# Up-projections of three MLPs in pairs of output tiles, by seven products of half tiles

## The chip, the cores and the metric

The kernel runs on one core of a Trainium2 chip. Its time is the device time of one execution in microseconds, as the median of several runs; less is better. The core has TensorE for matmuls, VectorE, ScalarE and GpSimd for elementwise work, and a queue on SyncE (SP) that issues the DMAs. Each engine takes its own instructions in order; engines wait for each other by semaphores.

## The reference, cut to what matters

Four layers, each a mixer (retention, convolution, gated linear attention, retention) and an MLP, with norms and residuals, on 512 tokens of 1024 features in float32:

```python
def sq_relu_mlp(u, w_up, w_down):
    return jnp.square(jax.nn.relu(u @ w_up)) @ w_down

h = x
for i in range(4):
    u = rmsnorm(h, norm_gains[i, 0])
    y = mixer(i, u)
    h = h + rmsnorm(y, norm_gains[i, 1])
    u = rmsnorm(h, norm_gains[i, 2])
    h = h + rmsnorm(sq_relu_mlp(u, mlp_w_up[i], mlp_w_down[i]), norm_gains[i, 3])
return h
```

Here w_up is 1024 x 4096 and w_down 4096 x 1024 in each layer.

## The kernel before

Activations lie transposed: features on the 128 partitions, the 512 tokens along the free axis. A 1024 x 512 activation is eight tiles of 128 x 512. For nearly the precision of float32, each operand is split into two tiles of type fp32r, hi (the value cast) and lo (the rest), and a product is three matmuls into one accumulator in PSUM: hi x hi, hi x lo, lo x hi (`mm3`, L392 to L394).

Weights come as panels of 128 x 1024, each the eight k-blocks of one output tile, in the order of use (`Stream`). `prep` loads a panel into a raw tile (L130, tag wraw, three buffers), casts it to hi on ScalarE (L137) and subtracts on VectorE for lo (L138). The ring of hi and lo tiles has six slots of each. `next` calls for panels up to three ahead.

In an MLP the 4096 hidden features are worked in four blocks of 1024 (b = 0 to 3). A block has eight up-projections, whose outputs become the eight tile pairs act, and then eight down-projections, which read all eight act pairs in order k = 0 to 7 and are added to the outputs y. An up-projection (`proj`) is 8 x 3 matmuls of 512 columns into one PSUM bank of seven. It is evacuated by `up`: VectorE takes the maximum with 0 times the norm factor r (L542), ScalarE squares (L543) and casts to hi (L373), VectorE subtracts for lo (L380). A down-projection is evacuated by ScalarE in block 0 (L246) and added by VectorE in the others (L251). Block 0 begins with four output tiles at once, in halves of 256 columns, while the norm is still being worked out (`lead`). Block 3 ends with four down-projections in halves of 256 columns (`trail`); their panels lie in four pairs of tiles of the MLP's own pool (tag w, eight buffers) instead of the ring, so that the next layer's panels can be cut early.

The operand X of the up-projections is h times a gain per feature, split into hi and lo by the `Close` of the mixer; the norm factor r comes in only at the evacuation. `tmp` tiles are a ring of four.

TensorE's instructions run in the order in which the program is written. Those of the other engines are ordered beforehand by a planner, which plays the program through in time: an instruction may be put ahead of earlier ones that are not ready. Tiles of a pool are released when their last reader is through.

Of the kernel before, what the change touches and what calls it, by code (L numbers as in the profile page):

```python
# [1 line left out]

# [1 line left out]

# [16 lines left out]
P = 128  # L21
# [72 lines left out]
class Stream:  # L94


    def __init__(self, K, src, ahead):
        self.K, self.src, self.ahead = K, src, ahead
        self.n = src.shape[0]
        self.ready, self.loaded, self.at = [], 0, 0  # L100
        self.aside = {}
        self.cut = {}

    def ring(self):
        K = self.K
# [1 line left out]

    def prep(self, parts=1):

        if self.loaded >= self.n:  # L110
            return []
        K = self.K
        nc = K.nc
        i = self.loaded
        self.loaded += 1
        if i in self.cut:
            hi, lo = self.aside.pop(i, self.ring)()
            pan = Panel(hi, lo)
            self.ready.append(pan)
            for tiles, src in zip((hi, lo), self.cut[i]):  # L120
                for t, x in enumerate(tiles):
                    nc.sync.dma_start(x.bitcast(F32), src[:, t * pan.w:(t + 1) * pan.w])
            return []
        raw = K.wp.tile([P, 8 * P], F32, name="wraw", tag="wraw", bufs=3)
        hi, lo = self.aside.pop(i, self.ring)()
        pan = Panel(hi, lo)
        self.ready.append(pan)

        def load(a, b):
            nc.sync.dma_start(raw[:, a:b], self.src[i][:, a:b])  # L130

        def split(a, b):
            for c in range(a, b, min(pan.w, b - a)):
                d = c + min(pan.w, b - a)
                t, o = divmod(c, pan.w)
                h, l = (x[t][:, o:o + d - c] for x in (hi, lo))
                nc.scalar.activation(h, raw[:, c:d], AF.Copy)  # L137
                nc.vector.tensor_tensor(l, raw[:, c:d], h.bitcast(F32), ALU.subtract)  # L138

        if parts == 1:  # L140
            load(0, 8 * P)
            split(0, 8 * P)
        else:
            w = 8 * P // parts
            return [(lambda a=a: load(a, a + w), lambda a=a: split(a, a + w)) for a in range(0, 8 * P, w)]

    def cut_early(self, i, pool):

        K = self.K
        nc = K.nc  # L150
        raw = K.wp.tile([P, 8 * P], F32, name="wraw", tag="wraw", bufs=3)
        nc.sync.dma_start(raw, self.src[i])
        hi, lo = (pool.tile([P, 8 * P], F32R, name="early", tag="early", bufs=2) for _ in range(2))
        nc.scalar.activation(hi, raw, AF.Copy)
        nc.vector.tensor_tensor(lo, raw, hi.bitcast(F32), ALU.subtract)
        self.cut[i] = [K.tc.dram_tile([P, 8 * P], F32, name=f"cut{n}{i}") for n in "hl"]
        for d, t in zip(self.cut[i], (hi, lo)):
            nc.sync.dma_start(d, t.bitcast(F32))

    def next(self, ahead=None):  # L160
        ahead = self.ahead if ahead is None else ahead
        while len(self.ready) < 1 + ahead and self.loaded < self.n:
            self.prep()
        self.at += 1
        return self.ready.pop(0)

# [3 lines left out]
            self.aside[self.at + first + i] = fn  # L170

    def fill(self, n):
        while len(self.ready) < n and self.loaded < self.n:
            self.prep()

    def group(self, n, ahead=0):
# [6 lines left out]
def _spare(pool, tag, bufs, w=8 * P):  # L183

    def alloc():
        return [[pool.tile([P, w], F32R, name=f"w{tag}", tag=tag, bufs=bufs) for _ in range(8 * P // w)] for _ in range(2)]
    return alloc
# [44 lines left out]
class Close:  # L232
# [26 lines left out]
    def half(self, c):  # L259
        K, nc = self.K, self.K.nc  # L260
        a, b = c
        if self.r is None:
            self.r = K.rp.tile([P, T], F32, name="ro", tag="ro", bufs=1)
            if self.nxt is not None:
                K.X = K.new_x()
        K.rsqrt(self.r, self.sum.mean(c), c)
        ts = {}
        with K.tc.manual_schedule(engines={DVE}):
            for k in range(KD + 2):
                if k < KD:  # L270
                    ts[k] = K.tmp()
                    nc.vector.scalar_tensor_tensor(ts[k][:, a:b], self.ys[k][:, a:b], K.gain(self.layer, self.which, k), self.r[:, a:b], ALU.mult, ALU.mult)  # L272
                if 1 <= k <= KD:
                    hk = K.h[k - 1][:, a:b]
                    nc.vector.tensor_tensor(hk, hk, ts[k - 1][:, a:b], ALU.add)  # L275
                    if self.nxt is None:
                        nc.sync.dma_start(K.out[(k - 1) * P:k * P, a:b], hk)
                    else:
                        K.split_hi(K.X[k - 1], hk, c, K.gain(*self.nxt, k - 1))
                if k >= 2 and self.nxt is not None:  # L280
                    K.split_lo(K.X[k - 2], K.h[k - 2][:, a:b], c, K.gain(*self.nxt, k - 2))
            if b == T and self.late:
                K.norm_sums()


class Kern:
# [99 lines left out]
        self.split_hi(pr, src, c, scale)  # L386
        self.split_lo(pr, src, c, scale)

    def mm3(self, out, A, B, start, stop):

        mm = self.nc.tensor.matmul
        mm(out, lhsT=A[0], rhs=B[0], start=start, stop=False)  # L392
        mm(out, lhsT=A[0], rhs=B[1], start=False, stop=False)  # L393
        mm(out, lhsT=A[1], rhs=B[0], start=False, stop=stop)  # L394
        self.tick(3 * (out.shape[-1] / 2400 + 0.0025))
# [122 lines left out]
            self.after(5.0 if c[1] == T else 2.5, lambda c=c: close.half(c))  # L518


    def mlp(self, close, early=()):
        nc = self.nc
        FB = 4
        early = list(early)
        steps = 0

        def step():

            nonlocal steps
            steps += 1  # L530
            if early and steps % 2 == 0:
                self.W.cut_early(early.pop(0), mp)

        with self.tc.tile_pool(name="mlp", bufs=1) as mp:
            self.W.keep(FB * 2 * KD - 4, [_spare(mp, "w", 8)] * 4)
            for b in range(FB):
                act = [self.pair(mp, "act", 2 * KD) for _ in range(KD)]

                def up(n, ps, c):
                    lo, hi = c  # L540
                    t = self.tmp()
                    nc.vector.scalar_tensor_tensor(t[:, lo:hi], ps[:, lo:hi], 0.0, self.r[:, lo:hi], ALU.max, ALU.mult)  # L542
                    nc.scalar.activation(t[:, lo:hi], t[:, lo:hi], AF.Square)  # L543
                    self.split(act[n], t[:, lo:hi], c)

                n0 = 0
                if b == 0:
                    n0 = 4
                    self.lead(n0, up)
                for n in range(n0, KD):  # L550
                    ps = self.proj()
                    self.when(lambda n=n, ps=ps: up(n, ps, (0, T)))
                    step()

                def down(n, ps, c):
                    if b == 0:
                        close.first(n, ps)
                    else:
                        close.add(n, ps, c)

                n1 = KD - 4 if b == FB - 1 else KD
                for n in range(n1):
                    down(n, self.proj(act), (0, T))
                    step()
                    if b == FB - 1:
                        close.done(n)
                if n1 < KD:
                    pan = self.W.group(4, 4)
                    self.trail([([pan[i].blk(k) for k in range(KD)], act, n1 + i) for i in range(4)], down, close)
# [794 lines left out]
    def run(self):  # L1364
        self.taps = [(0, 10)] * 2 + [(6, 10)] * 2 + [(7, 10)] * 2 + [(10, 8), (28, 0)]
        self.shift_at = 60.0
        self.side = 6
        self.fin = 2.0, 7.0, 7.0, 2.0
        self.ends = HALVES
        self.norm_at, self.tok_at = 22.0, 4.5  # L1370
        self.first_norm()
        for layer in range(DEPTH):
            kind, j = layer % 3, layer // 3
            close = Close(self, layer, 1, (layer, 2), True)
            if kind == 0:
                self.retention(layer, j, close)
            elif kind == 1:
                self.conv(layer, close)
            else:
                self.gla(layer, close)  # L1380
            last = layer + 1 == DEPTH
            early = range(self.W.at + N_MLP, self.W.at + N_MLP + N_CONV) if kind == 0 and not last else ()
            self.mlp(Close(self, layer, 3, None if last else (layer + 1, 0), not last and (layer + 1) % 3 == 0), early)
        self.flush()


# [136 lines left out]
```

## Time and profile before

| | us |
|---|---|
| median of 3 runs | 2761.25 |
| lowest and highest | 2756.51, 2762.49 |
| the profiled execution | 2758.31 |
| its span in the trace | 2756.6 |

| engine | busy us | share of the span | instructions |
|---|---|---|---|
| TensorE matmuls (PE) | 2695.5 | 98% | 13298 |
| TensorE weight loads (PEld) | 2277.9 | 83% | 13298 |
| VectorE (DVE) | 1637.7 | 59% | 2517 |
| ScalarE (ACT) | 1191.4 | 43% | 1801 |
| GpSimd (POOL) | 134.8 | 5% | 133 |

The shares are averages over stages with different limits. Weight loads run beside matmuls. The duration of one matmul in the trace contains the time it takes to drain, in which the next one already runs; how fast matmuls follow each other is read from their starts. An idle time is put down to the event that ended it.

### The profile page before, as it was taken

To read this page: it belongs to the slowest core of one execution; us is meant where nothing else is said; L and a number is where in the kernel's file an instruction comes from. 1 tells how busy PE (TensorE), PEld (TensorE's weight loads), DVE (VectorE), ACT (ScalarE), POOL (GpSimd) and SP (SyncE) were. 2 spreads that over 40 slices of the span, in tenths; PEclk is the share of its full clock that TensorE was granted. 3 is DMA by queue.
4 is the path that set the end of the run, shared out by engine and by line. 5 is a ranking of instruction groups with operands and counts; after the bars stand their busy time and mean duration, and the time that the engine had idled before them with its cause. 6 is when DMAs were issued, how large, how long until landed. Compare 5 with 4: busy or idle time off the path is not lost.

```text
span 2756.6 us, 33440 instructions
## 1 busy us (share of the span) xinstructions
PE 2695.5 (98%) x13298; PEld 2277.9 (83%) x13298; DVE 1637.7 (59%) x2517; ACT 1191.4 (43%) x1801; POOL 134.8 (5%) x133
## 2 busy tenths in 40 slices
PE   8999999999999699999999999999999999999998
PEld 7888888788898498888887888888888888988887
DVE  7755568455459974444688684345665555844444
ACT  5443445434337554332377554233443443543322
POOL 4000000000009400000000000000000000000000
PEclk9999999999999799999999999999999999999999
DMA  5222233766544003223122222323212222132231
GB/s 175 77 75 94 74 102 108 250 234 247 207 166 155 16 32 115 100 92 105 63 70 77 82 95 92 100 97 124 69 62 92 84 69 97 57 115 94 98 100 46
DMA packets 82670, 289.98 MB, mean 105 GB/s; under 512 B 9169, under 2 KB 11473, under 8 KB 82513
## 3 DMA queue, kind: packets, MB, share of 16 engines
q1 hardware_dynamic: 82368, 287.77, 30.9%
q8 instruction: 104, 1.70, 0.2%
q14 instruction: 54, 0.43, 0.0%
q10 hardware_dynamic: 144, 0.07, 0.0%
HBM read 260.02 MB, written 27.79 MB: 104 GB/s over the span
## 4 chain that ended last, share of the span: by engine, by line
PE 86%; DVE 8%; POOL 2%; ACT 2%; issue 1%; DMA 1%; SPq 0%; DVEq 0%; POOLq 0%; ACTq 0%
PE ps L393 28%; PE ps L394 28%; PE ps L392 28%; POOL y L897 2%; DVE wlo L138 1%; DVE ps L912 1%; DVE acc L210 1%; DMA wraw<-in_wst_dram 1%; DVE tmp L272 0%; DVE h L275 0%; PE st L218 0%; ACT whi L137 0%; DVE actl L380 0%; PE st L228 0%; DVE y L927 0%
## 5 line engine op out<-in xcount | busy, mean ns | idle before, releaser
L137 ACT ACTIVATE whi<-wraw 128x1024 fp32r<-128x1024 f32 (+1 forms) x396 | 414.3, 1049 | 820.3 <-PE ps L393 734.5
L392 PE MATMUL ps<-xh,whi 128*128 128x512 f32 (+1 forms) x1984 | 738.2, 372 | 3.9 <-DVE tmp L542 3.0
L393 PE MATMUL ps<-xl,whi 128*128 128x512 f32 (+1 forms) x1984 | 735.6, 371 | 1.1 <-DVE xl L382 1.1
L394 PE MATMUL ps<-xh,wlo 128*128 128x512 f32 (+1 forms) x1984 | 735.1, 371 | 0.0
L138 DVE TENSOR_TENSOR wlo<-wraw,whi 128x1024 fp32r<-128x1024 f32 (+1 forms) x396 | 483.3, 1223 | 218.3 <-ACT whi L137 213.6
L392 PEld LDWEIGHTS ps<-xh,whi 128*128 128x128 f32 x1984 | 374.9, 189 | 68.6 <-issue 3.8
L393 PEld LDWEIGHTS ps<-xl,whi 128*128 128x128 f32 x1984 | 374.8, 189 | 66.1 <-DVE xl L382 1.7
L394 PEld LDWEIGHTS ps<-xh,wlo 128*128 128x128 f32 x1984 | 374.9, 189 | 63.3
L393 PE MATMUL ps<-actl,whi 128*128 128x512 f32 x896 | 350.1, 391 | 1.4 <-DVE actl L380 1.3
L392 PE MATMUL ps<-acth,whi 128*128 128x512 f32 x896 | 349.0, 390 | 0.5 <-ACT acth L373 0.5
L394 PE MATMUL ps<-acth,wlo 128*128 128x512 f32 x896 | 348.9, 389 | 0.0
L251 DVE TENSOR_TENSOR y<-y,ps 128x512 f32<-128x512 f32 (+1 forms) x200 | 114.8, 580 | 319.0 <-PE ps L394 318.7
L542 DVE SCALAR_TENSOR_TENSOR tmp<-ps,rx 128x512 f32<-128x512 f32 x128 | 86.9, 689 | 227.2 <-PE ps L394 226.9
L393 PEld LDWEIGHTS ps<-actl,whi 128*128 128x128 f32 x896 | 168.3, 188 | 40.5 <-DVE actl L380 5.8
L392 PEld LDWEIGHTS ps<-acth,whi 128*128 128x128 f32 x896 | 168.3, 188 | 36.0 <-ACT acth L373 0.9
L394 PEld LDWEIGHTS ps<-acth,wlo 128*128 128x128 f32 x896 | 168.3, 188 | 34.0
L210 DVE TENSOR_TENSOR acc<-acc,sq 128x256 f32<-128x256 f32 (+1 forms) x245 | 118.6, 487 | 51.4 <-ACT sq L209 45.5
L392 PE MATMUL ps<-whi,xh 128*128 128x512 f32 (+1 forms) x384 | 138.3, 360 | 6.9 <-ACT whi L137 5.8
L393 PE MATMUL ps<-wlo,xh 128*128 128x512 f32 (+1 forms) x384 | 137.1, 357 | 0.0
L394 PE MATMUL ps<-whi,xl 128*128 128x512 f32 (+1 forms) x384 | 137.1, 357 | 0.0
L209 ACT ACTIVATE sq<-y 128x256 f32<-128x256 f32 (+1 forms) x105 | 46.9, 456 | 126.7 <-DVE y L251 105.0
L380 DVE TENSOR_TENSOR actl<-tmp,acth 128x512 fp32r<-128x512 f32 x128 | 87.6, 690 | 4.1 <-ACT acth L373 4.0
(321 smaller groups left out, 3835.7 us busy)
## 6 DMA issues: line engine op xcount, KB each, us to landing
wraw<-in_wst_dram SPq DMA_DIRECT2D x438, 512.0 KB, 3.5
cuth<-early SPq DMA_DIRECT2D x24, 512.0 KB, 2.6
cutl<-early SPq DMA_DIRECT2D x24, 512.0 KB, 3.0
whi<-cuth SPq DMA_DIRECT2D x20, 512.0 KB, 3.9
wlo<-cutl SPq DMA_DIRECT2D x20, 512.0 KB, 4.7
h<-in_xT_dram SPq DMA_DIRECT2D x8, 256.0 KB, 5.4
wraw<-in_wst_dram SPq DMA_DIRECT2D x8, 256.0 KB, 5.4
ww<-cuth SPq DMA_DIRECT2D x4, 512.0 KB, 6.3
```

The costliest lines, as they stand in the source:

```text
L137: nc.scalar.activation(h, raw[:, c:d], AF.Copy)
L138: nc.vector.tensor_tensor(l, raw[:, c:d], h.bitcast(F32), ALU.subtract)
L209: nc.scalar.activation(t, src, AF.Square, scale=scale)
L210: nc.vector.tensor_tensor(acc, acc, t, ALU.add)
L251: self.K.nc.vector.tensor_tensor(y, y, ps[:, a:b], ALU.add)
L380: self.nc.vector.tensor_tensor(lo, src, hi, ALU.subtract)
L392: mm(out, lhsT=A[0], rhs=B[0], start=start, stop=False)
L393: mm(out, lhsT=A[0], rhs=B[1], start=False, stop=False)
L394: mm(out, lhsT=A[1], rhs=B[0], start=False, stop=stop)
L542: nc.vector.scalar_tensor_tensor(t[:, lo:hi], ps[:, lo:hi], 0.0, self.r[:, lo:hi], ALU.max, ALU.mult)
L897: nc.gpsimd.tensor_tensor(co[i], co[i], o, ALU.add)
L912: nc.vector.scalar_tensor_tensor(sums[i], x, w, sums[i], ALU.mult, ALU.add)
```

## The change

In layers 1, 2 and 3 the up-projections of blocks 1 to 3 are made in pairs of output tiles. The two output tiles of 128 features and the 512 tokens make a 2 x 2 matrix of blocks (feature tile by half of the tokens), the 1024 input features are cut in two halves of four k-blocks, and the product of 2 x 2 blocks is made by seven products (Strassen's scheme, in Winograd's form) in place of eight. Each product has 4 k-blocks x 3 matmuls of 256 columns.

The operands: `combos` makes four combinations of the halves of X in block 0's down-phase, from h and the gain, and splits them into the eight tiles of tag w that the last four down panels also use. `Stream.pair` loads the two panels of a pair and makes the four combinations of their halves on VectorE; it gives four entries of the ring, three of two blocks each and one of one block, each cut into hi and lo. The first entry is cut at once, the others in `steps` as the stream is asked for them. `seven` asks for panels five ahead (`deep`), accumulates products into three PSUM banks where they are summed anyway, copies four partial sums out by ScalarE, adds by VectorE, and calls `up` with the sums in SBUF. `mm3` passes a flag that allows an accumulation to go on after its group was closed; that changes nothing in time by itself. `Close` also keeps the gain of X.

```diff
     def prep(self, parts=1):
+        if self.steps:
+            self.steps.pop(0)()
+            return []
         ...
         i = self.loaded
+        if i in self.pairs:
+            self.pair(i)
+            return []
...
+    def pair(self, i):
+        ...
+        H = 4 * P
+        r1 = pool.tile([P, 8 * P], F32, name="raw1", tag="raw1", bufs=2)
+        r2 = K.wp.tile([P, 8 * P], F32, name="wraw", tag="wraw", bufs=3)
+        nc.sync.dma_start(r1, self.src[i])
+        nc.sync.dma_start(r2, self.src[i + 1])
+        tt = nc.vector.tensor_tensor
+
+        def cut(raw, w=8 * P):
+            hi, lo = self.ring()
+            self.ready.append(Panel(hi, lo))
+            nc.scalar.activation(hi[0][:, :w], raw[:, :w], AF.Copy)
+            tt(lo[0][:, :w], raw[:, :w], hi[0][:, :w].bitcast(F32), ALU.subtract)
+
+        def second():
+            t = K.wp.tile([P, 8 * P], F32, name="wraw", tag="wraw", bufs=3)
+            tt(t[:, :H], r2[:, :H], r1[:, :H], ALU.subtract)
+            tt(t[:, H:], t[:, :H], r2[:, H:], ALU.subtract)
+            cut(t)
+            tt(r1[:, :H], r2[:, H:], r2[:, :H], ALU.subtract)
+            tt(r2[:, :H], t[:, H:], r1[:, H:], ALU.add)
+
+        cut(r1)
+        self.steps = [second, lambda: cut(r2), lambda: cut(r1, H)]
...
+    def combos(self, pool):
+        ...
+        def make(k):
+            xa, xb, s = self.tmp(), self.tmp(), self.tmp()
+            nc.scalar.activation(xa, self.h[k], AF.Identity, scale=self.gain(*self.X_gain, k))
+            nc.scalar.activation(xb, self.h[4 + k], AF.Identity, scale=self.gain(*self.X_gain, 4 + k))
+            tt(s[:, :H], xa[:, H:], xb[:, H:], ALU.add)
+            tt(s[:, H:], xa[:, :H], s[:, :H], ALU.subtract)
+            tt(xb[:, :H], xb[:, :H], s[:, H:], ALU.add)
+            tt(xb[:, H:], xa[:, :H], xa[:, H:], ALU.subtract)
+            c = (k % 2 * T, (k % 2 + 1) * T)
+            self.split(S12[k // 2], s, c)
+            self.split(S34[k // 2], xb, c)
...
+    def seven(self, evac):
+        ...
+        a, c, bd = self.ps(), self.ps(), self.ps()
+        e1, e2 = self.tmp(), self.tmp()
+        lo, hi = slice(0, H), slice(H, T)
+        ...
+        def entry():
+            W.fill(1 + W.deep)
+            return W.ready.pop(0)
+
+        w = entry()
+        product(1, a[:, lo], w, 0)
+        copy(e1[:, lo], a[:, lo])
+        product(2, bd[:, lo], w, 4)
+        w = entry()
+        product(5, c[:, lo], w, 0)
+        copy(e2[:, hi], c[:, lo])
+        product(6, a[:, lo], w, 4, True)
+        copy(e2[:, lo], a[:, lo])
+        w = entry()
+        product(4, bd[:, hi], w, 0)
+        product(3, c[:, lo], w, 4, True)
+        nc.vector.tensor_tensor(e2[:, lo], c[:, lo], e2[:, lo], ALU.add)
+        w = entry()
+        product(7, a[:, lo], w, 0, True)
+        copy(e1[:, hi], a[:, lo])
+        nc.vector.tensor_tensor(e2[:, hi], e1[:, hi], e2[:, hi], ALU.add)
+        evac(1, e2)
+        nc.vector.tensor_tensor(e1, bd, e1, ALU.add)
+        evac(0, e1)
+        W.at += 2
...
-    def mlp(self, close, early=()):
+    def mlp(self, close, early=(), seven=False):
...
+            if seven:
+                for b in range(1, FB):
+                    for n in range(0, KD, 2):
+                        self.W.pairs[self.W.at + b * 2 * KD + n] = mp
+                make = self.combos(mp)
...
+                if b and seven:
+                    for n in range(0, KD, 2):
+                        self.seven(lambda i, t: up(n + i, t, (0, T), t))
+                    n0 = KD
                 for n in range(n0, KD):
...
                 for n in range(n1):
                     down(n, self.proj(act), (0, T))
                     step()
+                    if b == 0 and seven and n % 2 == 0:
+                        make(n // 2)
...
-            self.mlp(Close(...), early)
+            self.mlp(Close(...), early, layer > 0)
```

## Rows read from the trace of the kernel before

**Rows 1.** Page, part 1: busy us (share of the span) and instructions.
```profile
PE 2695.5 (98%) x13298; PEld 2277.9 (83%) x13298; DVE 1637.7 (59%) x2517; ACT 1191.4 (43%) x1801; POOL 134.8 (5%) x133
```
**Rows 2.** Page, part 4: the chain that ended last, by engine.
```profile
PE 86%; DVE 8%; POOL 2%; ACT 2%; issue 1%; DMA 1%; SPq 0%; DVEq 0%; POOLq 0%; ACTq 0%
```
**Rows 3.** Windows, last MLP: us, busy by engine, granted clock, DMA share, GB/s.
```profile
2436.00:2480.00 44.00, 43.77 (x192) 35.49 (x191) 14.23 (x16) 15.74 (x22) 0.00 (x0) 1.00 0.28 95
2480.00:2524.00 44.00, 44.00 (x195) 36.45 (x195) 19.23 (x22) 17.07 (x23) 0.00 (x0) 1.00 0.29 97
2524.00:2568.00 44.00, 44.00 (x195) 36.43 (x194) 16.22 (x18) 10.13 (x11) 0.00 (x0) 1.00 0.29 96
```
**Rows 4.** Waits of TensorE and ScalarE, 2392 to 2743: us, times, longest.
```profile
PE ps L393 <- DVE actl L380: 0.2, 1, 0.2
...
ACT whi L137 <- PE ps L393: 165.6, 47, 4.4
```
**Rows 5.** Timeline, TensorE, an up-projection (start us, us): 21 matmuls from first to last.
```profile
2518.59 0.39 PE L392 MATMUL ps<-xh,whi 128*128 128x512 f32 x1
...
2523.35 0.39 PE L392 MATMUL ps<-xh,whi 128*128 128x512 f32 x1
```
**Rows 6.** Timeline, TensorE, the trail: 30 matmuls between; and its weight loads grouped.
```profile
2720.22 0.28 PE L392 MATMUL ps<-acth,ww 128*128 128x256 f32 x1
...
2723.82 0.28 PE L392 MATMUL ps<-acth,ww 128*128 128x256 f32 x1
...
L392 PEld LDWEIGHTS ps<-acth,ww 128*128 128x128 f32 x256 | 49.2, 192 | 0.3
```
**Rows 7.** Groups by form, 2590 to 2640: count | busy us, mean ns | idle before.
```profile
L138 DVE TENSOR_TENSOR wlo<-wraw,whi 128x1024 fp32r<-128x1024 f32 x10 | 12.3, 1226 | 1.8 <-ACT whi L137 1.8
...
L137 ACT ACTIVATE whi<-wraw 128x1024 fp32r<-128x1024 f32 x10 | 10.6, 1061 | 36.7 <-PE ps L393 36.7
...
L380 DVE TENSOR_TENSOR actl<-tmp,acth 128x512 fp32r<-128x512 f32 x5 | 3.5, 693 | 0.0
L542 DVE SCALAR_TENSOR_TENSOR tmp<-ps,rx 128x512 f32<-128x512 f32 x5 | 3.5, 692 | 13.5 <-PE ps L394 13.5
...
L373 ACT ACTIVATE acth<-tmp 128x512 fp32r<-128x512 f32 x5 | 3.2, 633 | 0.2
L543 ACT ACTIVATE tmp<-tmp 128x512 f32<-128x512 f32 x5 | 3.1, 618 | 0.0
```
**Rows 8.** Timeline, the kernel's end: instructions of 256 columns.
```profile
2744.01 0.42 ACT L209 ACTIVATE sq<-y 128x256 f32<-128x256 f32 x1 [1.65 <-DVE y L251]
2744.57 0.42 DVE L210 TENSOR_TENSOR acc<-acc,sq 128x256 f32<-128x256 f32 x1
```
**Rows 9.** Timeline, VectorE: back-to-back instructions merged (us of all).
```profile
2399.25 0.88 DVE L272 SCALAR_TENSOR_TENSOR tmp<-y,cst,ro 128x256 f32<-128x256 f32 x2
...
2413.92 2.36 DVE L138 TENSOR_TENSOR wlo<-wraw,whi 128x1024 fp32r<-128x1024 f32 x2 [1.65 <-ACT whi L137]
...
2429.18 2.48 DVE L542 SCALAR_TENSOR_TENSOR tmp<-ps,rx 128x512 f32<-128x512 f32 x4
```
**Rows 10.** Timeline, last up-projection of a block and the first down-projection.
```profile
2523.80 0.39 PE L394 MATMUL ps<-xh,wlo 128*128 128x512 f32 x1
2524.01 1.06 ACT L137 ACTIVATE whi<-wraw 128x1024 fp32r<-128x1024 f32 x1 [3.19 <-PE ps L393]
...
2524.23 0.69 DVE L542 SCALAR_TENSOR_TENSOR tmp<-ps,rx 128x512 f32<-128x512 f32 x1 [2.69 <-PE ps L394]
...
2524.97 0.62 ACT L543 ACTIVATE tmp<-tmp 128x512 f32<-128x512 f32 x1
2525.10 1.23 DVE L138 TENSOR_TENSOR wlo<-wraw,whi 128x1024 fp32r<-128x1024 f32 x1 [0.17 <-ACT whi L137]
...
2528.34 0.39 PE L393 MATMUL ps<-actl,whi 128*128 128x512 f32 x1
```
**Rows 11.** Page, part 6: DMA issues, KB each, median us to landing.
```profile
wraw<-in_wst_dram SPq DMA_DIRECT2D x438, 512.0 KB, 3.5
```

More of the change, by code (lines that the diff above doesn't have):

```diff
@@ L1 @@
 from contextlib import ExitStack
+from functools import partial
 import numpy as np
@@ L100, in __init__ @@
         self.ready, self.loaded, self.at = [], 0, 0
+        self.deep = 5
         self.aside = {}
         self.cut = {}
+        self.pairs, self.steps = {}, []
     def ring(self):
@@ L145, in prep @@
             return [(lambda a=a: load(a, a + w), lambda a=a: split(a, a + w)) for a in range(0, 8 * P, w)]
+    def pair(self, i):
+        K = self.K
+        nc = K.nc
+        pool = self.pairs.pop(i)
+        self.loaded += 2
+        H = 4 * P
[18 more added lines that the diff above has]
+        self.steps = [second, lambda: cut(r2), lambda: cut(r1, H)]
     def cut_early(self, i, pool):
@@ L161, in next @@
         ahead = self.ahead if ahead is None else ahead
-        while len(self.ready) < 1 + ahead and self.loaded < self.n:
-            self.prep()
+        self.fill(1 + ahead)
         self.at += 1
@@ L172, in fill @@
     def fill(self, n):
-        while len(self.ready) < n and self.loaded < self.n:
+        while len(self.ready) < n and (self.steps or self.loaded < self.n):
             self.prep()
@@ L264, in half @@
             if self.nxt is not None:
-                K.X = K.new_x()
+                K.X, K.X_gain = K.new_x(), self.nxt
         K.rsqrt(self.r, self.sum.mean(c), c)
@@ L387, in split, with mm3 @@
         self.split_lo(pr, src, c, scale)
-    def mm3(self, out, A, B, start, stop):
-        mm = self.nc.tensor.matmul
+    def mm3(self, out, A, B, start, stop, more=False):
+        mm = partial(self.nc.tensor.matmul, skip_group_check=more)
         mm(out, lhsT=A[0], rhs=B[0], start=start, stop=False)
@@ L518, in trail, with part @@
             self.after(5.0 if c[1] == T else 2.5, lambda c=c: close.half(c))
-    def mlp(self, close, early=()):
+    def combos(self, pool):
+        nc = self.nc
+        tt = nc.vector.tensor_tensor
+        H = T // 2
+        new = lambda: [pool.tile([P, 8 * P], F32R, name="wS", tag="w", bufs=8) for _ in range(2)]
+        S12, S34 = [new(), new()], [new(), new()]
+        def make(k):
[9 more added lines that the diff above has]
+            self.split(S34[k // 2], xb, c)
+        def part(S, which):
+            out = []
+            for k in range(4):
+                a = k % 2 * T + which * H
+                out.append(self.cut(S[k // 2], (a, a + H)))
+            return out
+        low, high = (0, H), (H, T)
+        self.S = {
+            1: [self.cut(self.X[k], low) for k in range(4)],
+            2: [self.cut(self.X[4 + k], low) for k in range(4)],
+            4: [self.cut(self.X[4 + k], high) for k in range(4)],
+            5: part(S12, 0), 6: part(S12, 1), 3: part(S34, 0), 7: part(S34, 1),
+        }
+        return make
@@ new lines, in seven, with product @@
+    def seven(self, evac):
+        nc = self.nc
+        H = T // 2
+        W = self.W
+        a, c, bd = self.ps(), self.ps(), self.ps()
+        e1, e2 = self.tmp(), self.tmp()
+        lo, hi = slice(0, H), slice(H, T)
+        def product(n, out, w, off, more=False):
+            S = self.S[n]
+            for k in range(4):
+                self.mm3(out, w.blk(off + k), S[k], k == 0 and not more, k == 3, more)
+        copy = lambda o, x: nc.scalar.activation(o, x, AF.Copy)
+        def entry():
[22 more added lines that the diff above has]
+        W.at += 2
@@ L535, in mlp, with up @@
             self.W.keep(FB * 2 * KD - 4, [_spare(mp, "w", 8)] * 4)
+            if seven:
[3 more added lines that the diff above has]
+                make = self.combos(mp)
             for b in range(FB):
                 act = [self.pair(mp, "act", 2 * KD) for _ in range(KD)]
-                def up(n, ps, c):
+                def up(n, ps, c, t=None):
                     lo, hi = c
-                    t = self.tmp()
+                    t = self.tmp() if t is None else t
                     nc.vector.scalar_tensor_tensor(t[:, lo:hi], ps[:, lo:hi], 0.0, self.r[:, lo:hi], ALU.max, ALU.mult)
@@ L1382, in run @@
             early = range(self.W.at + N_MLP, self.W.at + N_MLP + N_CONV) if kind == 0 and not last else ()
-            self.mlp(Close(self, layer, 3, None if last else (layer + 1, 0), not last and (layer + 1) % 3 == 0), early)
+            self.mlp(Close(self, layer, 3, None if last else (layer + 1, 0), not last and (layer + 1) % 3 == 0), early, layer > 0)
         self.flush()
```

## Prediction

> **What bounds the kernel now.** I read the page first: TensorE is busy 98% of the span [rows 1], and the chain of work that ended last runs through it for 86% [rows 2]. The windows over the last MLP come next: in 44 us TensorE is busy 43.77 to 44.00, at a granted clock of 1.00, while VectorE has 14.2 to 19.2 us and ScalarE 10.1 to 17.1 [rows 3]. The waits of that MLP agree: TensorE waits 0.2 us in all, and ScalarE's cast of a weight panel waits 47 times, 165.6 us in all, until TensorE gives a slot of the ring back [rows 4]. So in the MLPs nothing but the matmul stream sets the time; panels are cut as early as the six ring slots allow, not when the program asks for them. Last I read the timeline for the distance between matmuls, because a busy time of 390 ns overlaps its neighbours. Of 512 columns, 21 matmuls lie between 2518.59 and 2523.35: 4.76 / 21 = 0.2267 us each [rows 5]. Of 256 columns, 30 lie between 2720.22 and 2723.82: 0.1200 us each [rows 6].
>
> **Where the change applies.** The flag is layer > 0, so layers 1, 2 and 3 change, in blocks 1 to 3 of four: 9 blocks with 4 pairs each, 36 pairs. Retention, convolution, GLA, the first MLP, block 0 and all down-projections keep their matmuls.
>
> **TensorE, per pair.** Removed: 2 tiles x 8 k x 3 = 48 matmuls of 512 columns, 48 x 0.2267 = 10.88 us. Added: 7 products x 4 k x 3 = 84 of 256 columns, 84 x 0.1200 = 10.08 us [rows 5, 6]. Saved: 0.80 us; for 36 pairs 28.8 us. The columns fall by an eighth, but both distances hold about 13.4 ns beside the columns (226.7 less 512/2.4, 120.0 less 256/2.4), and 36 matmuls more pay that. A load of weights takes 192 ns, more than the 120 ns between two matmuls, but in the stretch of [rows 6] loads overlap and the distance is still 0.1200; those matmuls have the same shape and, as the new ones, a load each, so I take 0.1200. Bounds: at 0.1295 the saving is gone (10.88 / 84), and with loads one after the other it would be 0.192.
> The Trainium skill's page "TensorE: Matmul & The Clock Gate" (Back-to-back issue gap) puts a warm gap at N/2.4 + 2.5 ns, 109.2 ns for 256 columns. By it the new pair would take 9.17 us, 1.71 less than measured before, 61.6 us for all. The rows show 120.0 where it has 109.2, so the trace differs and decides.
>
> **Cutting the panels.** The loads stay two of 512 KB per pair, 3.5 us to landing [rows 11]. They are issued in the order of use on SP's queue; r1 has two tiles of its own and wraw keeps three slots, so a pair's loads can go out while the pair before is cut. Before, a pair cost two casts and two subtractions. Now: three full casts and a half one on ScalarE, three full subtractions and a half one on VectorE, and four VectorE sums of 512. With the spacing of VectorE's back-to-back instructions, 1.13 us for 1024 elements (2.36 less 1.23) and 0.60 for 512 ((2.48 less 0.69) / 3) [rows 9], that is 3 x 1.13 + 5 x 0.60 = 6.4 us of VectorE in place of 2.3. ScalarE: 3 x 1.06 + 0.63 = 3.8 us in place of 2.1 [rows 7].
>
> **Taking the products out.** ScalarE gets four copies of 256 columns (0.42 each [rows 8]), VectorE two sums of 256 (0.40 apart [rows 9]) and one of 512. The evacuation proper stays: two scalar_tensor_tensor and two lo subtractions on VectorE (4 x 0.60), two squares and two hi casts on ScalarE.
> VectorE per pair: 6.4 + 0.8 + 0.6 + 2.4 = 10.2 us, against 10.08 on TensorE. With whole durations, 1.23, 0.69 and 0.42, it is 3 x 1.23 + 10 x 0.69 + 2 x 0.42 = 11.4 us. ScalarE: 3.8 + 1.7 + 2.5 = 8.0. So in an up-phase VectorE goes from under half busy to full. What covers it is the ring: VectorE has more than 24 of 44 us free around a down-phase [rows 3], so five of the sixteen entries of the phase are cut before it begins, and the sums of the second pair too. What is left within its 40.3 us: cuts of 11 entries, with the sums of the last two pairs (3 x 1.13 less a half one for E6 to E8 = 2.9, then 2 x 6.4), five down panels (5.7), four evacuations (15.2, of which 3.4 fall behind the last product), one y sum: some 34 us in 40.3. It should keep up. Bounds of the lag at the phase's end: 0, or 4 x (11.4 less 10.08) = 5.3 us if nothing is cut ahead; I take 0, the side of [rows 4].
>
> **The end of an up-phase: the new wait.** The first down-projection needs act 0 to 7 in order; act 6 and 7 now both come out of the last pair, and both wait for its seventh product. Before, act 7 alone did, over three links. Say t = 0 at that product's end. In the trace the first instruction follows 0.04 us behind the last matmul, a change of engine costs 0.05, and the lo part of act 6 is read by a matmul 4.15 us behind that end (2528.34 less 2524.19) [rows 10]; its weight load, which holds the wait, comes 0.22 before it: 3.93. The new chain: copy 0.04 to 0.46; sum into e2 0.50 to 0.92; scalar_tensor_tensor for act 7 to 1.64; the e1 sum 1.57 to 2.26; scalar_tensor_tensor for act 6 2.29 to 2.98. On ScalarE meanwhile square and hi of act 7 to 2.97, then square and hi of act 6 to 4.31; its lo 4.34 to 5.03 [rows 7, 8]. Late by 1.1 us with the engines otherwise free.
> They are not free. In [rows 10] the cast of a panel starts at 2524.01, as the ring slot comes free and 0.18 us before the last product ends; its subtraction follows at 2525.10. With 256 columns that cast starts at -0.08, and the copy behind it at 0.88 instead of 0.04: 1.95 us late. If VectorE also takes the subtraction (0.98 + 0.04 to 2.16) before the sum into e2, the sum starts at 2.16 instead of 0.50: 2.75 us late. I take 1.95: the cast is in front by the row, but the subtraction of the panel before holds VectorE until about 0.8, and a sum that the program has first is then as likely to be next. Nine phase ends: 9 x 1.95 = 17.6 us; ends 9.9 and 24.8.
>
> **At nothing.** The combinations of X (four per layer, in block 0's down-phase): VectorE 4 x 0.42 + 2 x 0.69 = 3.1 us, ScalarE 4 x 0.63 = 2.5, once in two panels (10.9 us), beside TensorE's full stream with VectorE busy 14.2 of 44 [rows 3]; uncovered they would cost 12 x 5.6 = 67 us. They take the eight tiles of the last four down panels, which in blocks 3 can be cut only when the seventh product is through; TensorE reaches them four panels, over 20 us, later. In the sequence P1 P2 P5 P6 P4 P3 P7 a bank is written again 2.9 us after its last product (24 x 0.12), and the 0.42 us copy between has that long, behind at most one cast. Three banks per pair of seven, and two of four tmp tiles, leave a pair's time (10 us) for the evacuation.
>
> **Sum.** 28.8 less 17.6 is 11.2 us: 2758.31 of the profiled execution becomes 2747.1. The median of the three runs is 2.9 us above that execution; I forecast 2748, faster by 0.4%, its own range 2739 to 2757 (stalls of 9.9 to 24.8, and the 2.9).
>
> **Rivals.**
> 1. Slower: VectorE falls behind within the up-phase and the end pays. Place: the wait of the weight load of act 6 or 7, nine times. It decides from 28.8 / 9 = 3.2 us per phase. With whole durations and no head start the lag is 5.3, plus 1.1: 6.4 x 9 = 57.6, so 28.8 us slower, 2787. For it: VectorE's 10.2 to 11.4 against 10.08, and long links over ScalarE on both. Against it: idle time and the early cuts. 0.15.
> 2. No change: the middle of that, 2.6 to 3.8 us per phase, 5.5 us either side of before, 2753 to 2764. For it: every gap of the chain can be filled by a cast or subtraction of 1.06 to 1.23 us. 0.21.
> 3. The whole saving: cuts give way, or act 6 is out early enough, stall below 0.5 us: 2729.5 to 2734. Against it: the 1.1 us of the bare chain. 0.06.
> 4. The matmuls don't hold 0.1200, because loads, or the many short instructions, set the pace; at 0.192 a pair costs 16.1 us and the kernel 36 x 5.2 = 190 us more, 2948. Against it: 30 in a row at 0.1200. 0.02.
> 5. The short matmuls come closer together than in the rows: 106.7 of the 120.0 ns are columns at 2.4 GHz, the rest may shrink in a long stretch. At 0.109 a pair takes 9.16 us, 36 x 1.72 = 61.9 are saved, and with the 17.6 the time is 2714. Against it: neither distance of the trace shows it. 0.02.
> The page named above, of the Trainium skill, has such a gap in the section Back-to-back issue gap.
> The forecast itself has 0.54.
>
> **How the numbers follow.** No change means within 0.2%, 5.5 us, about what a measurement of this kernel can tell. Faster: the forecast except its upper end (0.52), the whole saving 0.06, closer matmuls 0.02: 0.60. Same: 0.21 and 0.02 of the forecast: 0.23. Slower: 0.15 and 0.02: 0.17. The range reaches from near the whole saving to the first third of the slow case: 2733 to 2768.
>
> **What would show it.** In the trace after, matmuls of 256 columns at 0.120 in the changed blocks and a pair in 10.1 us; TensorE's idle time before the weight load for act 6 or 7 in nine places of 1 to 3 us; VectorE about 85% busy in up-phases; a cast of a down panel just ahead of the last copy. I am wrong if TensorE waits inside the pairs (for a copy, a panel or a bank), if the nine waits are above 3.2 us, or if the distance of short matmuls differs from 0.120.

## The result, and the profile after

The kernel after takes 2780.64 us (median of 4 runs, 2777.49 to 2782.9), the kernel before 2760.88 beside it: ratio 1.0072, interval 1.006 to 1.0084. It is 19.8 us slower where 13 us faster were forecast, and above the range of 2733 to 2768. The rows here are those of the execution profiled (2779.93 us); line numbers moved: the three matmuls are L434 to L436, the cast and subtraction of a plain panel L146 and L147, those of a pair L175 and L176, the evacuation L669, L670, L415 and L422.

The page after, part 1 (busy us, share, instructions) and the chain that ended last, which answer to [rows 1] and [rows 2]:

```profile
PE 2688.8 (97%) x14594; PEld 2326.3 (84%) x14594; DVE 1867.3 (67%) x2913; ACT 1320.2 (48%) x2065; POOL 134.9 (5%) x133
...
PE 82%; DVE 9%; ACT 4%; POOL 2%; DMA 2%; issue 1%; DVEq 0%; POOLq 0%; ACTq 0%; SPq 0%
```

TensorE's busy time hardly fell; of the chain, ScalarE's part rose from 2% to 4% and VectorE's from 8% to 9%. The mean granted clock of the span fell from 0.992 to 0.985. TensorE's waits for the act tiles over the whole span (us, times, longest), before:

```profile
PE ps L393 <- DVE actl L380: 1.3, 5, 0.4
...
PE ps L392 <- ACT acth L373: 0.5, 1, 0.5
```

And after:

```profile
PE ps L434 <- ACT acth L415: 25.6, 13, 4.8
...
PE ps L435 <- DVE actl L422: 4.0, 13, 0.5
```

The matmuls did what was forecast. In an up-phase of the second layer, 35 steps from matmul to matmul lie between the starts below, 4.20 / 35 = 0.1200 us each, as in [rows 6] (timeline; the start and the duration in us):

```profile
1108.75 0.28 PE L434 MATMUL ps<-xh,whi 128*128 128x256 f32 x1
...
1112.95 0.28 PE L436 MATMUL ps<-wS,wlo 128*128 128x256 f32 x1
```

The end of the next up-phase is where time is lost. TensorE there, from the last product on:

```profile
1229.74 0.28 PE L436 MATMUL ps<-wS,wlo 128*128 128x256 f32 x1
1229.86 0.40 PE L434 MATMUL ps<-acth,whi 128*128 128x512 f32 x1
...
1233.74 0.39 PE L436 MATMUL ps<-acth,wlo 128*128 128x512 f32 x1
1236.03 0.50 PE L434 MATMUL ps<-acth,whi 128*128 128x512 f32 x1 [1.90 <-ACT acth L415]
1236.76 0.61 PE L435 MATMUL ps<-actl,whi 128*128 128x512 f32 x1 [0.23 <-DVE actl L422]
1237.17 0.63 PE L436 MATMUL ps<-acth,wlo 128*128 128x512 f32 x1
1237.60 0.63 PE L434 MATMUL ps<-acth,whi 128*128 128x512 f32 x1
```

Two steps from start to start are 2.29 and 0.73 us long instead of 0.227: the hi and lo tiles of act 6 come 2.57 us late together. Behind that the matmuls are 0.43 apart, not 0.227. The windows say why (from, to and length in us; busy us of TensorE's matmuls, its weight loads, VectorE, ScalarE, GpSimd; granted clock, DMA share, GB/s):

```profile
1229.00:1234.00 5.00, 5.00 (x27) 4.06 (x25) 4.75 (x8) 2.53 (x4) 0.00 (x0) 1.00 0.71 213
1234.00:1237.00 3.00, 0.88 (x3) 0.43 (x3) 2.04 (x3) 1.89 (x3) 0.00 (x0) 1.00 0.50 179
1237.00:1240.00 3.00, 3.00 (x8) 2.32 (x8) 0.88 (x2) 1.06 (x1) 0.00 (x0) 0.50 0.00 0
1240.00:1243.00 3.00, 3.00 (x13) 2.44 (x13) 2.39 (x3) 0.00 (x0) 0.00 (x0) 0.93 0.00 0
```

After the wait the granted clock is 0.50, the lower of its two levels, 1.2 GHz: 8 matmuls in 3 us where 13 go. In the kernel before the clock is 1.00 in the windows of [rows 3], and its trace has no fall in any of the three changed MLPs. ScalarE and VectorE at the same place show what act 6 waited for:

```profile
1229.94 1.06 ACT L146 ACTIVATE whi<-wraw 128x1024 fp32r<-128x1024 f32 x1 [0.38 <-PE ps L435]
1230.91 0.36 ACT L614 ACTIVATE tmp<-ps 128x256 f32<-128x256 f32 x1
```

```profile
1229.63 1.22 DVE L147 TENSOR_TENSOR wlo<-wraw,whi 128x1024 fp32r<-128x1024 f32 x1
1231.04 1.23 DVE L147 TENSOR_TENSOR wlo<-wraw,whi 128x1024 fp32r<-128x1024 f32 x1 [0.19 <-ACT whi L146]
1232.18 0.42 DVE L636 TENSOR_TENSOR tmp<-tmp 128x256 f32<-128x256 f32 x1
...
1236.01 0.69 DVE L422 TENSOR_TENSOR actl<-tmp,acth 128x512 fp32r<-128x512 f32 x1 [0.63 <-ACT acth L415]
```

The seventh product ends at 1230.02 (1229.74 and 0.28). The cast of a down panel starts 0.08 us ahead of that, the copy (L614) behind it 0.89 us after it, and VectorE takes that panel's subtraction before the sum (L636), which starts 2.16 us after it.

Block 3 is worse. Its end in the second layer, ScalarE:

```profile
1321.91 1.06 ACT L146 ACTIVATE ww<-wraw 128x1024 fp32r<-128x1024 f32 x1 [1.20 <-DMA wraw<-in_wst_dram]
1322.88 0.61 ACT L670 ACTIVATE tmp<-tmp 128x512 f32<-128x512 f32 x1
1323.52 0.63 ACT L415 ACTIVATE acth<-tmp 128x512 fp32r<-128x512 f32 x1
1324.37 1.06 ACT L146 ACTIVATE whi<-wraw 128x1024 fp32r<-128x1024 f32 x1 [0.22 <-DMA wraw<-in_wst_dram]
```

A cast into the tiles that the combinations of X had held (ww) is ahead in ScalarE's order and waits 1.20 us for its load, while the square of act 7 stands behind it; the next cast, ahead of the square of act 6, waits for a load too. From start to start TensorE has a step of 4.76 us there.

**The account.** All of it is read from the starts of matmuls in the two traces. From the last matmul of the phase before to the first of the phase behind, each of the nine up-phases takes 40.54 us in place of 43.75: 3.2 us less, as forecast, 28.9 in all. The nine down-phases behind them take 43.9 us more than before. For the one at the end shown above these are its windows, before and after:

```profile
1231.62:1274.91 43.29, 43.29 (x192) 35.87 (x191) 15.97 (x17) 9.62 (x10) 0.00 (x0) 1.00 0.30 98
```

```profile
1229.86:1277.48 47.62, 45.50 (x194) 36.93 (x192) 24.20 (x30) 10.86 (x13) 0.00 (x0) 0.96 0.20 66
```

Of the 43.9, 30.5 us are nine waits, counted beyond 0.227 a step: five of 2.57, one of 2.89, and 5.04, 5.54 and 4.23 in the three blocks 3. The other 13.3 us come right behind the waits. Behind two of them the clock stays, and 0.2 us are lost there each; behind the other seven it falls, and 1.4 to 2.6 are lost, 13.0 together. So the falls cost about 12 us. Three down-phases of block 0 take 1.2 us each more than before (45.40 in place of 44.19; see below): 3.6. So the three changed MLPs lose 43.9 + 3.6 - 28.9 = 18.6 us. The two executions profiled differ by 21.5 us; of the rest 2.2 lie in the GLA layer and 0.7 ahead of the second layer's MLP. The medians differ by 19.8.

### The profile page after: what moved, and what is told of

The parts are those of the page before. It is cut to its first block, busy times and chain, and to the rows that moved or that the text cites. A ratio compares the mean times of both kernels' runs of the same rounds, so it can differ in the third digit from the quotient of the medians.

```text
span 2778.1 us, 36840 instructions
## 1 busy us (share of the span) xinstructions
PE 2688.8 (97%) x14594; PEld 2326.3 (84%) x14594; DVE 1867.3 (67%) x2913; ACT 1320.2 (48%) x2065; POOL 134.9 (5%) x133
## 4 chain that ended last, share of the span: by engine, by line
PE 82%; DVE 9%; ACT 4%; POOL 2%; DMA 2%; issue 1%; DVEq 0%; POOLq 0%; ACTq 0%; SPq 0%
PE ps L435 27%; PE ps L434 27%; PE ps L436 27%; POOL y L1030 2%; DMA wraw<-in_wst_dram 2%; DVE wlo L147 1%; ACT whi L146 1%; DVE ps L1045 1%; DVE acc L252 1%; ACT tmp L670 1%; DVE tmp L314 0%; ACT acth L415 0%; DVE tmp L669 0%; DVE h L317 0%; PE st L260 0%
## 5 line engine op out<-in xcount | busy, mean ns | idle before, releaser
L434 PE MATMUL ps<-xh,whi 128*128 128x512 f32 (+1 forms) x1840 | 635.8, 346 | 4.2 <-DVE tmp L669 3.3
L435 PE MATMUL ps<-xl,whi 128*128 128x512 f32 (+1 forms) x1840 | 633.1, 344 | 1.1 <-DVE xl L424 1.1
L436 PE MATMUL ps<-xh,wlo 128*128 128x512 f32 (+1 forms) x1840 | 632.6, 344 | 0.0
L146 ACT ACTIVATE whi<-wraw 128x1024 fp32r<-128x1024 f32 (+1 forms) x324 | 337.5, 1046 | 392.5 <-PE ps L435 309.2
L147 DVE TENSOR_TENSOR wlo<-wraw,whi 128x1024 fp32r<-128x1024 f32 (+1 forms) x324 | 393.4, 1217 | 112.4 <-ACT whi L146 105.8
L434 PEld LDWEIGHTS ps<-xh,whi 128*128 128x128 f32 x1840 | 349.4, 190 | 46.9 <-issue 4.2
L436 PEld LDWEIGHTS ps<-xh,wlo 128*128 128x128 f32 x1840 | 349.4, 190 | 41.7 <-DVE wlo L147 0.3
L434 PE MATMUL ps<-acth,whi 128*128 128x512 f32 x896 | 355.5, 397 | 25.6 <-ACT acth L415 25.6
L436 PE MATMUL ps<-acth,wlo 128*128 128x512 f32 x896 | 353.6, 395 | 0.0
L434 PEld LDWEIGHTS ps<-acth,whi 128*128 128x128 f32 x896 | 171.5, 191 | 66.9 <-ACT acth L415 31.2
L436 PEld LDWEIGHTS ps<-acth,wlo 128*128 128x128 f32 x896 | 171.0, 191 | 35.1
L434 PE MATMUL ps<-wS,whi 128*128 128x256 f32 x576 | 163.0, 283 | 0.0
L435 PE MATMUL ps<-wS,whi 128*128 128x256 f32 x576 | 163.0, 283 | 0.0
L436 PE MATMUL ps<-wS,wlo 128*128 128x256 f32 x576 | 163.0, 283 | 0.0
L434 PE MATMUL ps<-whi,xh 128*128 128x512 f32 (+1 forms) x384 | 138.2, 360 | 6.9 <-ACT whi L146 5.8
L175 ACT ACTIVATE whi<-wraw 128x1024 fp32r<-128x1024 f32 x72 | 76.2, 1058 | 140.4 <-PE ps L435 122.8
L436 PE MATMUL ps<-whi,xl 128*128 128x512 f32 (+1 forms) x384 | 137.2, 357 | 0.0
```

The source lines that it names most:

```text
L175: nc.scalar.activation(hi[0][:, :w], raw[:, :w], AF.Copy)
```

## Experiments

Theory A: the saving is there, and what eats it lies at the ends of the up-phases: the late act 6, and the clock that falls behind the wait. Theory B, the rival of the prediction: VectorE lags through the whole phase. Theory C: the loss is spread, by another order of the planner.

**The last pair as plain up-projections.**

```diff
...
-                    for n in range(0, KD, 2):
+                    for n in range(0, KD - 2, 2):
                         self.seven(lambda i, t: up(n + i, t, (0, T), t))
-                    n0 = KD
+                    n0 = KD - 2
```

> The last pair of each changed block is made as two plain up-projections, as before; 27 pairs in place of 36. Theory A (the loss sits at the phase ends: act 6 and 7 come out late behind the last pair's long chain, and TensorE's clock falls after the wait): the nine waits go (under 3 us in all), no fall of the granted clock in the changed MLPs, and the time is before less 27 x 0.80 = 21.6 us, 2739. Theory B (VectorE falls behind through the whole phase, 1.3 us per pair): three pairs leave it about 4 us late, waits of 1 to 2 us stay at the nine ends: 2748 to 2760. Theory C (the loss is spread over the rest, by another order of the planner): above 2765.

2746.11 us, ratio 0.9946 (0.9929 to 0.9962): 14.2 us less than before, and 34.5 less than with the last pair in the scheme, though that pair's matmuls save 7.2. TensorE's waits from 1100 to 1345, which are those of the second layer's changed blocks, fell to 0.5 us:

```profile
PE ps L434 <- ACT acth L415: 0.3, 1, 0.3
PE ps L435 <- DVE actl L422: 0.2, 1, 0.2
```

The time alone lies between A's 2739 and the 2748 to 2760 of B. The trace speaks for A and against C: of the nine down-phases seven are as long as before, and no clock falls in the changed MLPs. 7.4 us of the 21.6 are missing. Of these 3.6 lie at block 0's ends as in the kernel after, and 3.3 in two down-phases of block 3, in the second and third layers, which are 1.5 and 1.8 us longer than before.

**Three down-projections side by side.**

```diff
+                m = 3 if b and seven else 0
+                if m:
+                    pan = self.W.group(m, self.W.ahead)
+                    pss = [self.ps() for _ in range(m)]
+                    for ks in (range(KD - 2), range(KD - 2, KD)):
+                        for i in range(m):
+                            for k in ks:
+                                self.mm3(pss[i], pan[i].blk(k), act[k], k == 0, k == KD - 1)
...
-                for n in range(n1):
+                for n in range(m, n1):
```

> All 36 pairs stay; the first three down-projections of a changed block run side by side, k = 0 to 5 of all three first, so that act 6 is needed 12.2 us after the phase's end, not 4.1. Theory A: the longest chain of the kernel after ended some 9 us behind the last product, so no wait is left, the clock stays at 2.4 GHz, and the whole saving of the matmuls shows: before less 28.8, 2732. Theory B: a lag of 5 to 6 us is hidden as well; it gives the same here and is told apart by the kernel without sums. Theory C: above 2755.

2735.82 us, ratio 0.991 (0.9895 to 0.9925): 24.5 less than before. In the changed blocks TensorE waits no more: their down-phases are as long as before to 0.03 us. 4.3 us of the 28.8 are missing; block 0's down-phases still take 45.40 us, and the kernel below with block 0 side by side finds most of them there.

**Without the sums of the panels.** The output differs, since the products are of other numbers.

```diff
         def second():
-            t = K.wp.tile([P, 8 * P], F32, name="wraw", tag="wraw", bufs=3)
-            tt(t[:, :H], r2[:, :H], r1[:, :H], ALU.subtract)
-            tt(t[:, H:], t[:, :H], r2[:, H:], ALU.subtract)
-            cut(t)
-            tt(r1[:, :H], r2[:, H:], r2[:, :H], ALU.subtract)
-            tt(r2[:, :H], t[:, H:], r1[:, H:], ALU.add)
+            cut(r2)
```

> The four VectorE sums that combine a pair's two panels are left out (the second panel is cut instead of the combination, so the products are of other numbers); VectorE's work per pair falls by 2.4 us, from 10.2 to 7.8, the matmuls stay. Theory B (lag over the phase): the lag goes, the waits at the ends fall below 1.5 us each, no fall of the clock: 2735 to 2745. Theory A (order of casts and subtractions at the phase's end): the chain behind the seventh product is the same, the six ends of blocks 1 and 2 still wait about 2.5 us each, the three of block 3 somewhat less than 4.2 to 5.5 because the raw tiles come free earlier, the clock still falls at most of them: 2768 to 2781.

2782.45 us, ratio 1.0079 (1.0064 to 1.0094): as slow as the kernel after, and 1.5 us above the range expected under A. VectorE did get its relief; here is the same up-phase (1104 to 1144) in the kernel after and without the sums (VectorE's busy time is the third column, 33.70 and 28.94):

```profile
1104.00:1144.00 40.00, 40.00 (x332) 39.88 (x332) 33.70 (x46) 26.72 (x45) 0.00 (x0) 1.00 0.47 141
```

```profile
1104.00:1144.00 40.00, 40.00 (x335) 39.96 (x335) 28.94 (x37) 27.65 (x44) 0.00 (x0) 1.00 0.41 121
```

TensorE is full in both, and all six ends of blocks 1 and 2 show the same two steps, 2.28 or 2.29 and 0.72 or 0.73 us. Theory B falls: VectorE's load over the phase does not make the wait. The time is not shorter for it, since TensorE now also waits inside the last pair of each block 3 for a copy (3.0 us in all), and the clock falls behind eight of the nine waits.

**Matmuls that nobody reads in place of the wait.**

```diff
         for k in range(ks):
+            if filler and k == 6:
+                st = self.st()
+                for _ in range(filler):
+                    self.nc.tensor.matmul(st, lhsT=p.blk(0)[0], rhs=self.X[0][0], start=True, stop=True)
...
-                    down(n, self.proj(act), (0, T))
+                    down(n, self.proj(act, KD, (20 if b == FB - 1 else 11) if b and seven and n == 0 else 0), (0, T))
```

> The kernel after with idle time filled: ahead of k = 6 of each changed block's first down-projection TensorE makes extra matmuls of 512 columns that nobody reads, 11 (2.5 us) in blocks 1 and 2, 20 (4.5 us) in block 3. They take the place of the wait. If the fall of the granted clock is caused by the idle time and costs time (theory A), the clock stays at 2.4 GHz through the changed MLPs and the kernel is faster than the kernel after by what the falls cost, 15 to 19 us, though it does more work: 2762 to 2766. If the falls cost nothing, or have another cause, it is as slow as the kernel after or slower: 2780 to 2785.

2767.46 us, ratio to before 1.0026 (1.0016 to 1.0036): 13.2 us faster than the kernel after (2780.64), with 126 matmuls more. They take 126 x 0.227 = 28.6 us, and with the 1.8 us of waits that are left about as long as the 30.5 of the kernel after, so the difference is put down to the clock. In the traces the three changed MLPs are 11.4 us shorter than in the kernel after, near the 12 of the account. The windows at the end shown above:

```profile
1233.00:1236.00 3.00, 3.00 (x15) 2.24 (x14) 2.11 (x4) 2.00 (x4) 0.00 (x0) 1.00 0.61 184
1236.00:1239.00 3.00, 3.00 (x14) 2.42 (x15) 1.48 (x2) 1.06 (x1) 0.00 (x0) 1.00 0.00 0
```

The clock stays at 1.00, no fall is left in the three changed MLPs, and the mean over the span is 0.992 again. The falls cost 11 to 13 us, less than the 15 to 19 expected, and the time is 1.5 us above its range. That idle time causes them is shown: where it is filled, they are gone.

**Side by side in block 0 too.** The kernel of three down-projections, with `m = 3 if seven` for every block.

> As the kernel with three down-projections side by side, but in block 0 of the changed MLPs too. There the combinations of X run on ScalarE and VectorE ahead of the evacuation of act 6 and 7, and TensorE waits about 1.6 us at each of the three block ends (0.4 in the kernel before). If that is why the side-by-side kernel saved 24.5 instead of 28.8, this one saves those 3 x 1.6 = 4.8 us more: 2731. If the rest of the saving went elsewhere (clock falls in the GLA layer, a slower stream of matmuls), it stays at 2736.

2730.89 us, ratio 0.9893 (0.9879 to 0.9908): 28.8 us less than before (25 to 33 by the interval). The trace holds the term of the matmuls closer: each of the three changed MLPs is 9.6 us shorter than before, 28.9 in all. Block 0's down-phases take 44.12 us in place of 45.40, which is 3.8 of the 4.3 that were missing. This version beats both kernels. From the first changed up-phase to the last block's end of the second layer's MLP TensorE is never idle:

```profile
1104.00:1345.00 241.00, 241.00 (x1583) 222.23 (x1583) 167.27 (x226) 114.12 (x173) 0.00 (x0) 1.00 0.35 108
```

What held act 7 up is in ScalarE's timeline of the kernel after, behind block 0's up-projections; TensorE waits there for its hi and its lo:

```profile
1060.91 0.71 ACT L573 ACTIVATE tmp<-h,cst 128x512 f32<-128x512 f32 x1
1061.53 0.61 ACT L670 ACTIVATE tmp<-tmp 128x512 f32<-128x512 f32 x1
1062.05 0.71 ACT L574 ACTIVATE tmp<-h,cst 128x512 f32<-128x512 f32 x1
1062.66 0.61 ACT L415 ACTIVATE acth<-tmp 128x512 fp32r<-128x512 f32 x1
```

```profile
1063.33 0.50 PE L434 MATMUL ps<-acth,whi 128*128 128x512 f32 x1 [0.22 <-ACT acth L415]
1064.33 0.50 PE L435 MATMUL ps<-actl,whi 128*128 128x512 f32 x1 [0.51 <-DVE actl L422]
```

The gains of the combinations (L573, L574), written into the down-phase, were put forward as soon as they were ready, between the evacuations of the last act tiles. That they are the cause is read from the timeline; a kernel that holds them back was not run.

**Casts kept away from the end.**

```diff
...
-                    down(n, self.proj(act), (0, T))
+                    ps = self.proj(act)
+                    if b and seven and n == 0:
+                        st = self.st()
+                        tiles = [t[0] for p in self.held for t in (p.hi, p.lo)]
+                        for t in tiles + (self.Stiles if b == FB - 1 else []):
+                            nc.tensor.matmul(st[:, :P], lhsT=t[:, :P], rhs=self.X[0][0][:, :P], start=True, stop=True)
+                    down(n, ps, (0, T))
```

Here `held` are the last two entries of the last pair and `Stiles` the tiles of the combinations of X.

> The kernel after, with the casts of down panels kept away from the phase's end: behind the first down-projection of each changed block a few matmuls of 128 columns, whose result nobody reads, read the ring slots of the last two entries (in block 3 also the eight tiles of the combinations of X), so that these slots come free only then; they add some 0.1 us each, 4 per block in blocks 1 and 2, 12 in block 3, about 6 us in all. If the casts and subtractions in front of the chain make the wait long (from 1.1 us for the bare chain to 2.6 in blocks 1 and 2 and 4 to 5.5 in block 3), all nine waits fall to 1.0 to 1.5 us, no fall of the granted clock is left in the changed MLPs, and the time is 2749 to 2756. If the chain itself is that long, the waits of blocks 1 and 2 stay near 2.6 and the time stays at 2776 to 2786.

2752.23 us, ratio 0.9971 (0.996 to 0.9983). All nine ends, block 3's too, now show steps of 0.6 and 0.73 us, 0.88 us late together, a little less than expected; no clock falls in the changed MLPs. VectorE at such an end (the sum L639 starts 0.77 us after the engine came free, with nothing in front of it but the copy L615 that it waits for):

```profile
1142.91 0.43 DVE L639 TENSOR_TENSOR tmp<-tmp 128x256 f32<-128x256 f32 x1 [0.77 <-ACT tmp L615]
1143.37 0.69 DVE L672 SCALAR_TENSOR_TENSOR tmp<-tmp,rx 128x512 f32<-128x512 f32 x1
```

The bare chain costs 0.9 us per end; what stood in front of it made 0.9 into 2.6 to 5.5.

## Why the prediction was wrong

**Right.** The distance of 0.1200 us and the 28.8 us; that VectorE keeps up within the phase; that TensorE waits for the lo and hi of act 6, nine times, and for nothing inside the pairs; the cast in front of the copy, 0.08 us ahead of the product's end; the bare chain (1.1 forecast, 0.9 measured).

**The term that was mis-sized: "Nine phase ends: 9 x 1.95 = 17.6 us".** It measured 30.5. In blocks 1 and 2 the far end of its bounds came true (2.75 forecast, 2.57 measured five times and 2.89 once): VectorE did take the subtraction first, and the sum started at 2.16 as worked out for that case. I took the middle because the subtraction before it would hold VectorE; [rows 10] had the pattern, an order in which whatever is ready goes in front, and no row spoke for the sum. In block 3 the bound itself was too low. "TensorE reaches them four panels, over 20 us, later" was true of those panels and missed the point: their casts stand in ScalarE's order in front of the last evacuation and wait there for their loads. The waits of block 3 were 4.2 to 5.5.

**What was left out: the clock.** The sum priced a wait at its length. With 30.5 in place of 17.6 it would have given 1.7 us slower than before. The rest is mostly the 11 to 13 us of matmuls at the lower clock behind seven waits, for which the sum had no term. The Trainium skill's page "TensorE: Matmul & The Clock Gate" (HAM oscillation — how this bites in real kernels) says of a kernel whose bursts of matmuls are parted by waits for DMA, of some 3 to 5 us, that each such wait sends the clock back to half. The trace agrees for the three waits of 4.2 to 5.5 us, and shows 0.50 behind four of the six shorter ones too. I had not weighed that page.

**"At nothing. The combinations of X".** VectorE and ScalarE had the time, but not at the place where the planner put them: 3.6 us in the three blocks 0.

The rival that forecast slower (2787) came near the measured time for another reason; its mechanism, the lag, is refuted by the kernel without sums.

**Left open.** The GLA layer, which the change does not touch, takes 2.2 us longer in the trace of the kernel after, and 1.5 to 3.4 us longer in those of the six experiments. The kernel after has two falls of the clock there that the profiled execution of before has not, at waits of TensorE that both have (one of 2.97 us in both, one of 1.95 before and 2.52 after). Of the nine waits of the changed blocks two of 2.57 us had no fall behind them, with the same idle time as others; what decides was not tried.

## What to carry to other kernels

Where matmuls become cheaper and their results come out of a longer chain, look at the first reader behind the stage, and work its order so that it needs the last results last: three output tiles side by side turned 19.8 us lost into 28.8 saved. In a plan that fills every gap, count each ready instruction as in front of the chain, those that wait for a load too. Price idle time of TensorE at more than its length when matmuls follow it.

## What the hardware showed beyond that

Waiting cost some 40% more than its own length: over the changed MLPs 30.5 us of it brought 11 to 13 us more through matmuls at the lower clock, and 126 matmuls without a reader made the kernel 13.2 us faster. Matmuls of 256 columns kept 0.1200 us over whole up-phases although a load of weights takes 0.19 us: 336 of them in the 40.32 us from 1277.70 to 1318.02.
